# New rates and operand waits in the clock that paces a mixer's background work

## The chip, the cores and the metric

The kernel runs on one core of one Trainium2 chip. A core has a matrix engine (TensorE, PE in the rows), a vector engine (VectorE, DVE), a scalar engine (ScalarE, ACT), a general engine (GpSimd, POOL) and a queue that only issues transfers (SyncE, SP). Each engine works through its own instructions strictly in the order in which the program lists them, and waits on semaphores for the others. [...] The metric is the time of one execution in microseconds (us) on the device, the median of several runs.

## The reference, cut to what matters

One layer works on 256 frames of width 2048, in float32:

```
x = x + 1/2 * SwiGLU_1(RMSNorm(x))                  # D_FF = 5632
p = RMSNorm(x) @ W_in                               # one projection for both groups of heads
x = x + concat(rwkv7_mix(p), hgrn2_mix(p)) @ W_out
x = x + 1/2 * SwiGLU_2(RMSNorm(x))
out = RMSNorm(x)
```

`rwkv7_mix` (16 heads of 64) is a delta-rule recurrence over the frames, `S = S*w + sa (kk*a) + v k` with `sa = -S kk`, followed by a norm over each head, a bonus and a gate. `hgrn2_mix` (8 heads of 128) is a gated linear recurrence, followed by a norm over each head and a gate. Both run forward in time.

## The kernel before, in words

**Weights.** Every large product is float32 work made of float32r products. A weight tile of 128x1024 ("piece", 678 of them, 512 KB each) is loaded into `raw`, ScalarE casts it to `hi`, and `lo = raw - hi` is made by VectorE or by GpSimd. TensorE then runs 8 products of `hi` with 512 columns and 8 of `lo` with 256 columns into a tile `mm`. Four buffers each for `raw`, `hi` and `lo`; the split of a piece is listed five pieces ahead of its use. Pieces 0 to 263 are SwiGLU 1, 264 to 381 the projections of the mixer, 382 to 413 the output projection `W_out`, 414 to 677 SwiGLU 2.

**The mixer.** The recurrences don't wait for the whole projection. Four generators do them: `rwkv(hf)` for two halves of the RWKV heads (groups 0 and 1) and `hgrn(gi)` for two halves of the HGRN heads. A group of RWKV first makes its decays, keys and score tiles; then it solves a triangular system by 31 steps of two VectorE instructions each, the second of which needs the first (`state["chain"]`); then it passes four chunks of 64 frames, in which TensorE products and PSUM copies follow one another (product of the state and scores, copy by ScalarE, product with the inverse, copy by VectorE, update of the state, output); then come the norm over each head (two sums by TensorE, a square root, four reciprocals), the bonus (an addition by GpSimd), the gate and `put_y`, which leaves the operand of `W_out`. Their products go to tiles `ps` and stand on TensorE's queue between the large products.

**What sets the order.** The program is listed by a loop over units of one piece. After each unit, `poll` (line 311) lets the first two generators go on by one step, if their delay in ticks is over and if `max(V.until, S.until) <= model.now() + BEHIND` (line 313, BEHIND is 2500 ns). `V`, `S` and `G` wrap the engines: every call adds a cost to the engine's `until`, and notes when its output will be `ready`. `model.now()` is TensorE's own count of columns. `need` (line 186) holds a generator until the operands of its next products are ready by that count. `spare` (line 398) uses the two `until` values to give a `lo` to VectorE or to GpSimd. The pieces of `W_out` need the generators' results: `yop` (line 1000) and `add_acc` (line 1010) call `step_bg` over and over while a result isn't there, which makes every generator go on at once, without a large product between. Afterwards the framework's own scheduler may still move instructions past one another where data and buffers allow it.

Of the kernel before, what the change touches and what calls it, by code (L numbers as in the profile page):

```python
# [97 lines left out]
def names_of(xs):  # L98
    return [getattr(getattr(x, "tensor", x), "name", None) for x in xs if hasattr(x, "shape")]


class Model:

    RATE = {"vector": 1.04, "scalar": 0.83, "gpsimd": 2.6}
    FIXED = {"vector": 90, "scalar": 110, "gpsimd": 60, "tensor": 3}
    LATENCY = 200.0

    def __init__(self):  # L110
# [10 lines left out]
class Engine:  # L121
# [3 lines left out]
    def cost(self, op, n):  # L125
        rate = self.model.RATE[self.name]
        if op == "reciprocal":
            rate *= 6
        elif self.name == "vector" and op in ("tensor_copy", "tensor_scalar"):
            rate *= 0.6  # L130
        elif self.name == "gpsimd" and op == "memset":
            rate *= 0.2
        elif op == "dma_start":
            return 1000.0
        return self.model.FIXED[self.name] + rate * n

# [3 lines left out]
    def __getattr__(self, op):  # L140
        fn = getattr(self.engine, op)

        def call(*args, **kwargs):
            m = self.model
            cost = self.cost(op, math.prod(args[0].shape[1:]))
            begin = max(self.until, m.now())
            self.until = begin + cost
            done = max(begin, m.wait(*args)) + cost + m.LATENCY + (5000.0 if op == "dma_start" else 0.0)
            for n in names_of(args[:1]):
                m.ready[n] = done  # L150
            return fn(*args, **kwargs)  # L151

        return call
# [1202 lines left out]
```

## Time and profile before

| | |
|---|---|
| median of 3 runs | 2068.35 us (2067.53 to 2068.65) |
| the profiled execution | 2067.46 us, its span 2065.7 us |
| TensorE busy | 2023.5 us, 98% of the span |
| VectorE, ScalarE, GpSimd busy | 1375.6, 1010.6, 362.3 us |
| `lo` subtractions on VectorE and GpSimd | 615 and 70 in the trace |

The span is the time from the first to the last instruction. A busy time is the time in which an engine had an instruction in work. Where rows carry a bracket, it is the idle time ahead of them and what ended it. All helper calls share two lines, L151 (the wrapped engines) and L171 (the products), so rows are told apart by their tiles: `mm` are the large products, `ps` the generators' products, `t` most working tiles. A tile `t` or `b` in the rows stands for many buffers.

### The profile page before, as it was taken

How to read it: one execution, taken by the hardware profiler on the slowest of the kernel's cores; microseconds unless marked ns; L12 is line 12 of the kernel's file. 1: busy time of each engine (PE TensorE's matmuls, PEld its weight loads, DVE VectorE, ACT ScalarE, POOL GpSimd, SP SyncE). 2: the span in 40 equal slices, each digit the busy share in tenths (PEclk: the TensorE clock that was granted, in tenths of full speed). 3: DMA queues.
4: the chain of work that ended last, by engine and by line, in shares of the span. 5: the costliest groups of instructions: out<-in, count | busy, mean ns of one | idle time of the engine just before them, and what ended most of it. 6: DMA issues, size and time to landing. Idle time of an engine off the chain costs nothing.

```text
span 2065.7 us, 31617 instructions
## 1 busy us (share of the span) xinstructions
PE 2023.5 (98%) x12766; PEld 1764.1 (85%) x12766; DVE 1375.6 (67%) x1498; ACT 1010.6 (49%) x1199; POOL 362.3 (18%) x220
## 2 busy tenths in 40 slices
PE   9999999999999999999989899999999999999998
PEld 7888888888888888788868788888888888888887
DVE  7665565565556688986888668856555655555657
ACT  6444443444344466465556545544444344434434
POOL 1211110111011032322343104211111011101101
PEclk9999999999999999999999999999999999999999
DMA  7555555556555565443434435555555555555553
GB/s 260 194 187 191 187 186 191 190 188 190 187 188 189 186 229 177 153 135 126 131 117 150 148 111 177 192 189 188 184 193 188 189 188 190 188 190 187 190 187 120
DMA packets 106146, 368.33 MB, mean 178 GB/s; under 512 B 11632, under 2 KB 18032, under 8 KB 105744
## 3 DMA queue, kind: packets, MB, share of 16 engines
q1 hardware_dynamic: 104352, 359.97, 53.2%
q0 software_dynamic: 1104, 6.06, 0.8%
q8 instruction: 100, 1.64, 0.3%
q14 instruction: 46, 0.38, 0.1%
q10 hardware_dynamic: 544, 0.28, 0.0%
HBM read 362.08 MB, written 4.19 MB: 177 GB/s over the span
## 4 chain that ended last, share of the span: by engine, by line
PE 49%; DVE 3%; POOL 1%; issue 1%; ACT 0%; DVEq 0%; POOLq 0%; ACTq 0%
PE mm L171 45%; PE ps L171 4%; DVE t L151 2%; POOL t L151 1%; DVE lo L151 1%; ACT t L151 0%; DVE xts L151 0%; DVE b L151 0%; POOL lo L151 0%; PE ps L175 0%; POOL b L151 0%; ACT hi L151 0%; DVEq L1352 0%; ACT inv L151 0%; ACT itok L151 0%
## 5 line engine op out<-in xcount | busy, mean ns | idle before, releaser
L171 PE MATMUL mm<-t,hi 128*128 128x512 f32 x5264 | 1332.7, 394 | 3.7 <-DVE t L151 3.5
L151 ACT CAST hi<-raw 128x1024 fp32r<-128x1024 f32 (+1 forms) x685 | 711.1, 1040 | 882.6 <-PE mm L171 752.3
L171 PEld LDWEIGHTS mm<-t,hi 128*128 128x128 f32 x5264 | 948.5, 190 | 174.9 <-ACT hi L151 2.2
L151 DVE TENSOR_TENSOR lo<-raw,hi 128x1024 fp32r<-128x1024 f32 (+1 forms) x615 | 777.0, 1265 | 443.0 <-ACT hi L151 420.4
L171 PEld LDWEIGHTS mm<-t,lo 128*128 128x128 f32 x5296 | 727.7, 191 | 69.9 <-POOL lo L151 11.4
L171 PE MATMUL mm<-t,lo 128*128 128x256 f32 x5296 | 749.2, 284 | 13.0 <-POOL lo L151 10.5
L151 POOL TENSOR_TENSOR lo<-raw,hi 128x1024 fp32r<-128x1024 f32 x70 | 170.4, 2434 | 531.9 <-ACT hi L151 508.3
L151 POOL TENSOR_TENSOR t<-t,inv 128x1024 f32<-128x1024 f32 x22 | 53.0, 2407 | 777.8 <-ACT t L151 777.8
L151 DVE TENSOR_TENSOR t<-t,t 128x512 fp32r<-128x512 f32 (+25 forms) x243 | 171.6, 710 | 13.9 <-ACT t L151 7.6
L151 DVE TENSOR_TENSOR t<-mm,t 128x512 f32<-128x512 f32 x122 | 83.3, 683 | 88.9 <-ACT t L151 88.9
L151 DVE SCALAR_TENSOR_TENSOR xts<-mm,xts 128x512 f32<-128x512 f32 x126 | 86.6, 688 | 76.3 <-PE mm L171 75.9
L151 ACT COPY t<-mm 128x512 f32<-128x512 f32 x122 | 70.8, 580 | 16.2 <-DVE t L151 14.9
L151 ACT CAST t<-t 128x512 fp32r<-128x512 f32 x72 | 44.1, 622 | 27.2 <-DVE t L151 18.9
L151 DVE TENSOR_TENSOR t<-t,inv 128x1024 f32<-128x1024 f32 (+1 forms) x35 | 44.1, 1261 | 1.0
L151 DVE RECIPROCAL t<-t 128x256 f32<-128x256 f32 x24 | 41.4, 1737 | 2.4 <-ACT t L151 2.3
L151 ACT ACTIVATE t<-t 128x1024 f32<-128x1024 f32 (+2 forms) x32 | 32.9, 1028 | 12.8 <-DVE t L151 12.8
L151 POOL TENSOR_TENSOR t<-t,t 128x1024 f32<-128x1024 f32 (+1 forms) x9 | 25.4, 2820 | 73.2 <-ACT hi L151 45.0
L151 DVE SCALAR_TENSOR_TENSOR t<-xts,vec,t 128x256 fp32r<-128x256 f32 x48 | 25.9, 561 | 13.9 <-ACT t L151 13.9
L151 ACT ACTIVATE t<-xts,vec 128x256 fp32r<-128x256 f32 x48 | 23.0, 505 | 22.0 <-DVE xts L151 19.1
L151 ACT COPY t<-ps 32x512 f32<-32x512 f32 (+8 forms) x44 | 19.7, 447 | 27.4 <-PE ps L171 26.4
L171 PE MATMUL mm<-hi,t 128*128 128x512 f32 x128 | 32.4, 393 | 0.0
L151 ACT ACT_TABLE_LOAD x21 | 26.9, 1283 | 5.0 <-DMA xts<-in_xt_dram 3.4
(134 smaller groups left out, 713.6 us busy)
## 6 DMA issues: line engine op xcount, KB each, us to landing
raw<-in_ffn_w_up_dram SPq DMA_DIRECT2D x176, 512.0 KB, 3.4
raw<-in_ffn_w_down_dram SPq DMA_DIRECT2D x176, 512.0 KB, 3.3
raw<-in_ffn_w_gate_dram SPq DMA_DIRECT2D x173, 512.0 KB, 3.4
raw<-in_w_in_dram SPq DMA_DIRECT2D x96, 512.0 KB, 3.4
raw<-in_w_out_dram SPq DMA_DIRECT2D x32, 512.0 KB, 3.3
raw<-in_w_i_dram SPq DMA_DIRECT2D x16, 512.0 KB, 3.3
raw<-in_w_lora_dram SPq DMA_DIRECT2D x6, 512.0 KB, 3.4
spill<-xts POOLq DMA_DIRECT2D x1, 2048.0 KB, 10.1
```

Of the source, the lines that this page charges most:

```text
L151: return fn(*args, **kwargs)
L171: return self.engine.matmul(out, a, b, **kwargs)
```

## The change

The clock of VectorE, ScalarE and GpSimd is changed in three ways. The rates and fixed costs have other numbers; `tensor_reduce`, `tensor_tensor_scan` and `transpose` get their own factors, `tensor_copy` loses its discount, and a reduction is counted by its input. And a call (other than a transfer) now begins, in the clock, no sooner than its operands are ready, so that `until` takes in the wait; before, the wait only moved the output's `ready`. Nothing of the arithmetic is changed.

```diff
-    RATE = {"vector": 1.04, "scalar": 0.83, "gpsimd": 2.6}
-    FIXED = {"vector": 90, "scalar": 110, "gpsimd": 60, "tensor": 3}
+    RATE = {"vector": 1.1, "scalar": 0.87, "gpsimd": 2.4}
+    FIXED = {"vector": 130, "scalar": 160, "gpsimd": 100, "tensor": 3}
...
-            rate *= 6
-        elif self.name == "vector" and op in ("tensor_copy", "tensor_scalar"):
+            rate *= 5.7
+        elif op in ("tensor_reduce", "tensor_tensor_scan"):
+            rate *= 2
+        elif self.name == "vector" and op == "transpose":
+            rate *= 1.3
+        elif self.name == "vector" and op == "tensor_scalar":
             rate *= 0.6
...
-            cost = self.cost(op, math.prod(args[0].shape[1:]))
+            cost = self.cost(op, math.prod(args[op == "tensor_reduce"].shape[1:]))
+
             begin = max(self.until, m.now())
+            if op != "dma_start":
+                begin = max(begin, m.wait(*args[1:], *kwargs.values()))
             self.until = begin + cost
```

What the change moves is seen in the engines' own lists. The added lines shift the helper lines by seven (L151 is now L158, L171 is L178).

TensorE, group 1 of RWKV, where its triangular system is solved. `xts` holds the scores here, the first operand of the two 32x32 groups is the transposed result of the 31 steps, and each `mm` row is half of a piece's `hi` or `lo`. Before:

```order
L171 MATMUL ps<-t_10506,xts 32x32 x32
L171 MATMUL mm<-t_6148,lo 128x256 x2
L171 MATMUL mm<-t_6203,hi 128x512 x4
L171 MATMUL mm<-t_6255,hi 128x512 x4
L171 MATMUL mm<-t_6203,lo 128x256 x4
L171 MATMUL mm<-t_6255,lo 128x256 x4
L171 MATMUL mm<-t_6312,hi 128x512 x4
L171 MATMUL ps<-q_10446,t_10445 64x64 x4
L171 MATMUL ps<-q_10446,t_10445 64x65 x4
L171 MATMUL mm<-t_6364,hi 128x512 x4
L171 MATMUL mm<-t_6312,lo 128x256 x2
L171 MATMUL ps<-t_10507,t_10548 32x32 x32
```

And now:

```order
L178 MATMUL mm<-t_11103,lo 128x256 x4
L178 MATMUL mm<-t_11106,lo 128x256 x4
L178 MATMUL ps<-t_11171,xts 32x32 x32
L178 MATMUL ps<-t_11172,t_11175 32x32 x32
L178 MATMUL ps<-b_11077,xts 64x64 x8
L178 MATMUL ps<-t_11267,t_11100 64x64 x8
L178 MATMUL ps<-b_11077,b_10968 64x64 x8
L178 MATMUL ps<-xts,b_11077 64x64 x8
L178 MATMUL ps<-st_103,b_10763 64x128
```

Before, large products of the projection stand between these groups, at piece 374 and after it. Now they stand inside the output projection, behind pieces 398 and 399, and no large product follows until the gate of group 1 is through: 72 rows of `ps` with 224 products in a row. Before, the longest such run within the mixer has 37 products.

TensorE, group 0 of RWKV, at its gate (`t_6647` is the gate's activation). Before:

```order
L171 MATMUL mm<-t_6364,hi 128x512 x2
L171 MATMUL ps<-t_6647,t_6872 128x256 x4
L171 MATMUL ps<-t_6647,t_8377 128x256 x4
L171 MATMUL mm<-t_6364,hi 128x512 x2
```

And now, with the levels of group 1 of HGRN (`q`) ahead of the gate, and behind it the first large product that needs group 0's result (`t_10526`):

```order
L178 MATMUL ps<-t_6647,t_9939 128x256 x5
L178 MATMUL ps<-q_9281,t_10166 32x32 x32
L178 MATMUL ps<-q_10264,t_10263 32x32 x32
L178 MATMUL ps<-q_10311,t_10310 32x32 x32
L178 MATMUL ps<-q_10358,t_10357 32x32 x32
L178 MATMUL ps<-q_10405,t_10404 32x32 x32
L178 MATMUL ps<-q_10459,t_10458 32x32 x12
L178 MATMUL ps<-q_10459,t_10458 32x33 x4
L178 MATMUL ps<-t_6647,t_6908 128x256 x2
L178 MATMUL ps<-t_6647,t_9812 128x256 x2
L178 MATMUL mm<-t_10526,hi 128x512 x6
```

This is the end of a second such run, 60 rows with 284 products, at piece 383 (before, the gate of group 0 stood at piece 340, in the projections).

GpSimd, the end of the mixer. `xts` is now the residual, which comes back by a transfer from `spill` and takes four additions; the last row here is the bonus of RWKV group 1 (`t_10686` before, `t_11252` now). Before:

```order
L151 DMA xts<-spill 128x4096
L151 TENSOR_TENSOR xts<-t_11036,xts 128x1024
L151 TENSOR_TENSOR xts<-t_11205,xts 128x1024
L151 TENSOR_TENSOR lo<-raw,hi 128x1024
L151 TENSOR_TENSOR xts<-t_11326,xts 128x1024
L151 TENSOR_TENSOR t_10686<-t_10686,t_9702 128x1024
```

And now:

```order
L158 DMA xts<-spill 128x4096
L158 TENSOR_TENSOR t_11464<-t_11459,t_11464 128x2x256
L158 TENSOR_TENSOR xts<-t_10573,xts 128x1024
L158 TENSOR_TENSOR xts<-t_10683,xts 128x1024
L158 TENSOR_TENSOR xts<-t_10793,xts 128x1024
L158 TENSOR_TENSOR xts<-t_10927,xts 128x1024
L158 TENSOR_TENSOR t_11252<-t_11252,t_10894 128x1024
```

All four additions, where three stood before, are now ahead of the bonus. Over the whole program 110 `lo` subtractions move from VectorE to GpSimd (180 of them are listed there now, 70 before), most in the two SwiGLU stages, where GpSimd now makes four of every 16 pieces of gate and up (mostly two before) and one of every three of down (mostly one of 24 before).

## Rows read from the trace of the kernel before

**Rows 1.** Busy time by stage: stretch, length, then each engine, clock, DMA share, GB/s

```profile
800.00:1300.00 500.00, 472.12 (x3873) 398.86 (x3872) 406.43 (x540) 287.46 (x390) 152.87 (x114) 0.98 0.43 142
1300.00:2040.00 740.00, 740.00 (x4240) 651.22 (x4240) 450.15 (x427) 333.56 (x356) 92.31 (x39) 1.00 0.58 187
```

**Rows 2.** What TensorE waited for from 800 to 1300 us: total, times, longest

```profile
PE ps L171 <- DVE t L151: 11.0, 7, 6.8
PE mm L171 <- POOL lo L151: 10.5, 2, 6.9
```

**Rows 3.** Timeline of TensorE around its longest wait: start, length, instruction

```profile
1051.39 2.00 PE L171 MATMUL mm<-t,hi 128*128 128x512 f32 x8
1060.25 2.08 PE L171 MATMUL mm<-t,lo 128*128 128x256 f32 x8 [6.86 <-POOL lo L151]
1062.12 3.52 PE L171 MATMUL mm<-t,hi 128*128 128x512 f32 x8
1065.48 1.12 PE L171 MATMUL mm<-t,lo 128*128 128x256 f32 x8
```

**Rows 4.** Timeline of TensorE, products of one chunk of RWKV

```profile
1210.34 0.43 PE L171 MATMUL ps<-st,b 128*64 128x128 f32 x2
...
1211.97 0.40 PE L171 MATMUL ps<-b,xts 128*64 128x64 f32 x4
...
1213.20 1.14 PE L171 MATMUL ps<-t,t 64*64 64x64 f32 x16
...
1218.42 0.69 PE L171 MATMUL ps<-b,b 128*64 128x64 f32 x16
...
1221.29 0.34 PE L171 MATMUL ps<-xts,b 128*64 128x64 f32 x4
```

**Rows 5.** Groups of instructions by shape, 800 to 1300 us: count | busy, mean ns | idle

```profile
L151 DVE RECIPROCAL t<-t 128x256 f32<-128x256 f32 x24 | 41.4, 1737 | 2.4 <-ACT t L151 2.3
...
L151 POOL TENSOR_TENSOR t<-t,t 128x1024 f32<-128x1024 f32 x8 | 23.5, 2935 | 72.4 <-ACT hi L151 45.0 <-ACT t L151 14.2 <-DVE t L151 12.8
L151 DVE TENSOR_TENSOR t<-t,t 128x512 fp32r<-128x512 f32 x27 | 22.3, 851 | 7.8 <-ACT t L151 7.6
...
L151 ACT ACT_TABLE_LOAD x13 | 16.7, 1283 | 0.2
L151 ACT CAST t<-t 128x512 fp32r<-128x512 f32 x27 | 16.2, 623 | 11.7 <-POOL t L151 3.5 <-DVE b L151 3.5 <-DVE t L151 3.4
...
L151 POOL TENSOR_SCALAR t<-t,vec 128x256 f32<-128x256 f32 x16 | 13.9, 874 | 28.4 <-ACT t L151 20.2 <-DVE t L151 7.5 <-ACT hi L151 0.6
...
L151 ACT ACTIVATE t<-t 128x1024 f32<-128x1024 f32 x8 | 8.5, 1062 | 3.9 <-DVE t L151 3.8
...
L151 DVE COPY b<-ps 64x512 f32<-64x512 f32 x8 | 5.5, 689 | 4.3 <-PE ps L171 4.2
...
L151 ACT COPY t<-ps 64x512 f32<-64x512 f32 x8 | 4.6, 579 | 7.3 <-PE ps L171 7.3
```

**Rows 6.** Groups by shape, VectorE, 1128 to 1148 us: steps of the triangular solve

```profile
L151 DVE TENSOR_TENSOR t<-t,t 128x126 f32<-128x126 f32 x5 | 1.5, 291 | 0.1
...
L151 DVE TENSOR_TENSOR t<-t,t 128x16 f32<-128x16 f32 x2 | 0.3, 167 | 0.0
```

**Rows 7.** Timeline of GpSimd at the end of the mixer

```profile
1233.86 0.59 POOL L151 DMA_DIRECT2D xts<-spill  x1 [13.33 <-PE ps L171]
1242.40 5.97 POOL L151 TENSOR_TENSOR xts<-t,xts 128x1024 f32<-128x1024 f32 x2 [7.95 <-DMA xts<-spill]
...
1265.71 3.28 POOL L151 TENSOR_TENSOR t<-t,t 128x1024 f32<-128x1024 f32 x1 [5.45 <-DVE t L151]
```

**Rows 8.** Timeline of GpSimd and VectorE in SwiGLU 2

```profile
1431.51 2.41 POOL L151 TENSOR_TENSOR t<-t,inv 128x1024 f32<-128x1024 f32 x1 [24.12 <-ACT t L151]
...
1432.88 2.12 DVE L151 TENSOR_TENSOR lo<-raw,hi 128x1024 fp32r<-128x1024 f32 x1 [1.41 <-ACT hi L151]
...
1435.67 1.23 DVE L151 TENSOR_TENSOR lo<-raw,hi 128x1024 fp32r<-128x1024 f32 x1 [0.67 <-ACT hi L151]
```

## The prediction

> **What bounds the kernel now.** I first read busy time by stage. From 1300 to 2040 us TensorE is busy 740.00 of 740 us at full clock [rows 1]: the SwiGLU stages are TensorE and nothing else, and no reordering can make them shorter. From 800 to 1300 us, the mixer, it is busy 472.12 of 500 us, so 27.9 us are idle there. That is all an ordering clock can win back in the middle. The list of what TensorE waited for names the idle time: 11.0 us for a VectorE result of the generators (one wait of 6.8, the end of a triangular solve) and 10.5 us in two waits for a `lo` on GpSimd [rows 2]. The timeline shows that a long wait costs more than its length: after the 6.86 us gap eight `lo` products took 2.08 us instead of 1.12 and eight `hi` products 3.52 instead of 2.00, so TensorE ran at half clock and lost another 2.5 us [rows 3].
>
> **What the change moves.** The clock now holds VectorE's and ScalarE's `until` further ahead of TensorE's, since it takes in waits. `poll` lets a generator go on only while `until` is at most 2500 ns ahead, so the generators are let on less often, and everything of them comes later in the lists. The listing shows how late: the chunks of group 0 no longer stand in the projections but at piece 383, the solve and chunks of group 1 behind pieces 398 and 399. There the output projection needs the results, and the generators are driven to their end with no large product between: two runs, of 284 and 224 products of `ps`. A serial chain that lay beside large products now lies on TensorE's path. The question is what each costs.
>
> **A chunk.** State and score products run from 1210.34 to 1212.37, the inverse's take 1.14, the update's 0.69, the output's about 2.5, up to 1221.63 [rows 4]; between them stand a ScalarE copy of 0.58 and a VectorE copy of 0.69 [rows 5]. In series: 2.0 + 0.6 + 1.1 + 0.7 + 0.7 + 2.5 = 7.7 us, of which TensorE works 6.4; the last chunk, without the update, 7.0 and 5.7. So the chunks themselves idle TensorE by only 1.3 us each. The norms and the solve are dearer.
>
> **Run A, group 0 at piece 383.** Two chunks without large products: 14.7 us, TensorE 12.1. Then the norm, on one path: three table loads of ScalarE (3.9, one for group 1's square root that stands ahead), two wide passes (2.1), four casts (2.5), two splits (1.7) and six reciprocals (10.4, two of them group 1's) make 20.6 us [rows 5]. Behind them VectorE lists group 1's and HGRN's work, and GpSimd three 128x1024 products (8.8, the bonus last) and four of the scalings (3.5) [rows 5], with about eight level products of HGRN, 7 by an estimate at the 0.87 of a scaling: 19 us. Then a level, the gate's products, four VectorE products and the last split, all short: I take 8. Elapsed 14.7 + 20.6 + 19 + 8 = 62 us. TensorE has the two chunks and some 12 us of sums, levels and gate (an estimate: some ten groups of small products, each about the 1.1 us of the inverse's): 24. Idle: 38 us.
>
> **Run B, group 1 behind piece 399.** From the last scores: two reciprocals of HGRN (3.5 [rows 5]) and the copies and the transpose ahead of the solve (4, an estimate of six passes at the 0.6 to 0.7 of the copies in [rows 5]); 62 steps between 0.29 and 0.17 us [rows 6], 16 us by a mean of 0.26, with two splits (1.7) and one `lo` (1.2, [rows 8]) among them; transposes, two block products and copies, 8 by an estimate of a dozen such passes. That is 34 us. Four chunks: 4.7 for the first, which has no state, 7.7, 7.7 and 7.0, so 27. Then the norm: one wide pass, four casts, two splits, four reciprocals (1.1 + 2.5 + 1.7 + 7.0, [rows 5]) and 8 for sums, subtraction, root and scaling (again a dozen such passes): 20 us. Beside it GpSimd brings back the residual: the transfer can start when the last chunk has let go of the buffer, takes 8.5 us to its first use and then 3.0 us an addition [rows 7]. Four additions are now listed ahead of the bonus, so the bonus starts 0.6 + 8 + 12 = 20.6 us after the chunks, no later than the norm lets it; bonus 2.9, then gate and split 3. So 27 us. In all 34 + 27 + 27 = 88 us. TensorE has two pieces (16 products each at 740/4240 us, 5.6 us in all, [rows 1]), two block products (2.5), chunks (22) and sums with gate (5): 35. Idle: 53 us.
>
> **Clock.** Four gaps in these runs are longer than the 6.86 us after which half clock was seen: the norm of A, the start and the middle of the solve, the norm of B. At 2.5 us each, 10 us [rows 3].
>
> **What is won.** With steps held back longer, the projections run with fewer waits. Of the 27.9 us idle and of some 7 us of half clock after three large gaps I take 20 as gone: the 6.8 us wait for a solve has moved into the runs, one of two waits for a `lo` goes, and half of the small ones. The bounds are 35 (all gone) and 0, since GpSimd's list in the projections has the same pattern as where a `lo` came late (a `lo` behind eight scalings and two wide products) and twice as many `lo`.
>
> **The moved `lo`.** In a slice of SwiGLU, 16 pieces at 2.79 us or 44.6 us, GpSimd now has four `lo` and one product, five times 2.41 [rows 8]: 12 us. `hi` is cast four pieces ahead of use, so a `lo` that takes 1.2 us longer is early by several us still: 0. If the cover were gone, it would be 1.2 us for each of 110, 130 us; if VectorE's time were the bound, a gain. Neither is, with TensorE at 740 of 740. There is one price beside it: a `lo` on VectorE took 2.12 us instead of 1.23 while GpSimd ran a product [rows 8]. [...] In SwiGLU it changes nothing; in run B the additions may hold the norm's splits.
>
> The edits of the rates alone have no cost of their own: they act through the order only, as above.
>
> **Sum.** Profiled execution 2067.5 us + 38 + 53 + 10 - 20 = 2148.5 us. It lies 0.9 us below the median of the runs, within their spread; I say 2148 us.
>
> **Rivals.**
> 1. Only one run is exposed. The scheduler moved two pieces into run B; if VectorE and GpSimd run so far ahead of TensorE that A's norm is mostly done when TensorE comes to it, A's 38 us and two clock losses fall away: 2148 - 43 = 2105 us. For it: TensorE has 12 us of large products among A's first chunks. Against: TensorE's queue is in order, and the norm needs the last chunk's output. 12%.
> [...]
> 3. Not slower. The place is the middle: all of the 35 us are won, and each run idles TensorE by no more than the chunk copies and half of the solve, about 5 and 12 us, with one clock loss of 2.5: 2067 - 35 + 20 = 2052 us. It decides if the two runs together idle TensorE less than 35 us; my count is 91, and the norm's reciprocals alone are 7 us each in series. 4%.
> 4. It doesn't do what it says: the order hardly changes, 2068 us. The lists above exclude most of it. 1%.
>
> **How the numbers follow.** The forecast holds 65%, rival 1 12%, rival 2 18%, rivals 3 and 4 5%. The range of the likeliest comes from the won time (0 to 35, against 20), the estimates in the runs (27 us in all, by a third either way) and clock (5 to 15): 2125 to 2178. For 8 in 10 I reach to both neighbours: 2098 to 2188. A measurement of this kernel tells about 0.2%, 4 us, from no change. Faster by more: 0.03; within: 0.02; slower: 0.95.
>
> **What would show it.** In the profile after, TensorE should have two stretches after 1100 us with no large product, of about 62 and 88 us, busy for some 24 and 35 us of them, with half clock in parts; its waits should name VectorE's `t` and GpSimd's `t` or `xts`, and the critical chain should run through reciprocals and the solve's small products. The projections should have less idle time than 27.9 us. SwiGLU 2 should stay at 100% with GpSimd busier (some 190 to 215 us of 740, 47 more `lo` at 2.41 us on top of 92). I am wrong if TensorE is busy in both runs, or if a SwiGLU stage shows waits for a `lo` on GpSimd.

## The result, and the profile after

The kernel after takes 2155.61 us (median; 2153.70 to 2162.46), the one before 2068.19: a ratio of 1.0431, with a 95% interval of 1.0418 to 1.0444. 2148 us was forecast, with a range of 2098 to 2188. From the page before, and the head of the page after:

```profile
PE 2023.5 (98%) x12766; PEld 1764.1 (85%) x12766; DVE 1375.6 (67%) x1498; ACT 1010.6 (49%) x1199; POOL 362.3 (18%) x220
```

```profile
span 2152.8 us, 31657 instructions
PE 2052.7 (95%) x12766; PEld 1789.2 (83%) x12766; DVE 1274.2 (59%) x1383; ACT 1015.4 (47%) x1202; POOL 631.0 (29%) x335
PEclk9999999999999999999996875899999999999999
```

TensorE runs the same 12766 instructions, but is busy 2052.7 us where it was 2023.5. Nothing was added to it, so the 29.2 us more are the same products at a lower granted clock (0.965 of full speed on average, 0.993 before). Its idle time is 2152.8 - 2052.7 = 100.1 us; before it was 2065.7 - 2023.5 = 42.2. So the 87.1 us of span are 57.9 of idle time and 29.2 of clock. The stretches show where (columns as in [rows 1]):

```profile
800.00:1130.00 330.00, 321.18 (x2302) 276.10 (x2302) 250.70 (x294) 189.69 (x240) 105.46 (x73) 0.98 0.52 168
1130.00:1205.00 75.00, 46.99 (x632) 34.48 (x630) 52.04 (x66) 38.24 (x64) 34.40 (x34) 0.68 0.05 14
1205.00:1256.00 51.00, 49.71 (x321) 43.26 (x321) 31.86 (x38) 27.70 (x38) 7.57 (x4) 1.00 0.44 145
1256.00:1365.00 109.00, 62.07 (x502) 51.13 (x501) 55.79 (x112) 25.32 (x39) 23.87 (x15) 0.61 0.09 30
1365.00:2040.00 675.00, 675.00 (x3868) 594.02 (x3867) 369.81 (x346) 312.29 (x341) 192.42 (x80) 1.00 0.57 187
```

The second and the fourth row are the two runs: 28.0 and 46.9 us idle, at mean clocks of 0.68 and 0.61, with almost no transfers (5% and 9% of the DMA engines). The projections ahead of them have 8.8 us of idle time, against 27.9 in the mixer before [rows 1], and SwiGLU 2 is full. What TensorE waited for from 1130 to 1380 us names the engines:

```profile
PE mm L178 <- DVE t L158: 23.9, 4, 11.4
PE ps L178 <- ACT t L158: 21.6, 13, 6.3
PE ps L178 <- DVE t L158: 18.0, 4, 13.9
PE ps L178 <- POOL q L158: 7.5, 2, 4.4
```

The long waits are for results of the generators, two of them for the `t` that the output projection itself reads (`mm`). No wait for a `lo` is left among them. TensorE's timeline, first across run A, then across run B:

```profile
1135.10 0.74 PE L178 MATMUL mm<-t,lo 128*128 128x256 f32 x4
...
1178.51 1.08 PE L178 MATMUL ps<-q,t 128*32 128x32 f32 x64 [6.27 <-ACT t L158]
...
1189.42 1.08 PE L178 MATMUL ps<-q,t 128*32 128x32 f32 x64 [4.41 <-POOL q L158]
...
1202.30 2.56 PE L178 MATMUL mm<-t,hi 128*128 128x512 f32 x10 [0.75 <-DVE t L158]
...
1269.58 3.50 PE L178 MATMUL mm<-t,hi 128*128 128x512 f32 x8 [11.24 <-DVE t L158]
...
1290.72 1.92 PE L178 MATMUL ps<-t,xts 32*32 32x32 f32 x64 [13.89 <-DVE t L158]
...
1296.66 1.97 PE L178 MATMUL ps<-b,xts 128*64 128x64 f32 x16
...
1308.17 1.14 PE L178 MATMUL ps<-t,t 64*64 64x64 f32 x16 [0.72 <-ACT t L158]
1310.09 1.08 PE L178 MATMUL ps<-b,b 128*64 128x64 f32 x16 [0.78 <-DVE b L158]
...
1318.68 1.14 PE L178 MATMUL ps<-t,t 64*64 64x64 f32 x16 [0.71 <-ACT t L158]
...
1337.44 2.17 PE L178 MATMUL ps<-t,bones_r 128*128 128x512 f32 x4 [1.12 <-ACT t L158]
...
1360.71 3.78 PE L178 MATMUL mm<-t,hi 128*128 128x512 f32 x8 [11.44 <-DVE t L158]
```

From the last large product before run A (ending at 1135.8) to the next are 66.5 us; from the last scores (1258.3) to the large products behind run B 102.4 us. A chunk goes every 10.5 us (1308.17 to 1318.68), and its update took 1.08 us where [rows 4] have 0.69. The eight `hi` products behind the two long waits of `mm` take 3.50 and 3.78 us, at a granted clock of 0.57 (1269.58 to 1273.10) and 0.50 (1360.70 to 1364.50). Behind the gap of [rows 3] it was 0.50 (1060.25 to 1065.40).

The end of run B on VectorE, then on GpSimd, answers to [rows 5, 7]:

```profile
1344.80 6.59 DVE L158 RECIPROCAL t<-t 128x256 f32<-128x256 f32 x4 [1.83 <-ACT t L158]
...
1352.68 3.28 DVE L158 TENSOR_SCALAR t<-t,vec 128x256 f32<-128x256 f32 x4
```

```profile
1336.63 0.57 POOL L158 DMA_DIRECT2D xts<-spill  x1 [43.63 <-PE ps L178]
...
1344.62 10.23 POOL L158 TENSOR_TENSOR xts<-t,xts 128x1024 f32<-128x1024 f32 x4 [0.49 <-DMA xts<-spill]
1356.11 2.34 POOL L158 TENSOR_TENSOR t<-t,t 128x1024 f32<-128x1024 f32 x1 [1.26 <-DVE t L158]
```

The four additions are done at 1354.85, 1.3 us before the bonus can start: the bonus waits for VectorE, not for the residual itself. The last section shows what the additions did to VectorE.

### The profile page after: what moved, and what is told of

The parts are those of the page before. It is cut to its first block, busy times and chain, and to the rows that moved or that the text cites. A ratio compares the mean times of both kernels' runs of the same rounds, so it can differ in the third digit from the quotient of the medians.

```text
span 2152.8 us, 31657 instructions
## 1 busy us (share of the span) xinstructions
PE 2052.7 (95%) x12766; PEld 1789.2 (83%) x12766; DVE 1274.2 (59%) x1383; ACT 1015.4 (47%) x1202; POOL 631.0 (29%) x335
## 5 line engine op out<-in xcount | busy, mean ns | idle before, releaser
L178 PE MATMUL mm<-t,hi 128*128 128x512 f32 x5264 | 1330.9, 394 | 27.8 <-DVE t L158 27.3
L158 ACT CAST hi<-raw 128x1024 fp32r<-128x1024 f32 (+1 forms) x685 | 710.8, 1040 | 913.9 <-PE mm L178 865.2
L178 PEld LDWEIGHTS mm<-t,hi 128*128 128x128 f32 x5264 | 950.7, 190 | 200.0 <-DVE t L158 27.8
L158 DVE TENSOR_TENSOR lo<-raw,hi 128x1024 fp32r<-128x1024 f32 (+2 forms) x505 | 639.3, 1268 | 480.9 <-ACT hi L158 470.0
L178 PEld LDWEIGHTS mm<-t,lo 128*128 128x128 f32 x5296 | 725.2, 191 | 62.4 <-DVE lo L158 5.6
L178 PE MATMUL mm<-t,lo 128*128 128x256 f32 x5296 | 744.2, 283 | 7.5 <-DVE lo L158 3.9
L158 POOL TENSOR_TENSOR lo<-raw,hi 128x1024 fp32r<-128x1024 f32 x180 | 437.9, 2433 | 900.0 <-ACT hi L158 889.6
L158 DVE TENSOR_TENSOR t<-mm,t 128x512 f32<-128x512 f32 x122 | 83.5, 685 | 185.3 <-ACT t L158 185.2
L158 DVE TENSOR_TENSOR t<-t,t 128x512 f32<-128x512 f32 (+24 forms) x238 | 169.5, 715 | 17.7 <-ACT t L158 10.4
L158 DVE SCALAR_TENSOR_TENSOR xts<-mm,xts 128x512 f32<-128x512 f32 x126 | 86.9, 690 | 76.8 <-PE mm L178 74.8
L158 POOL TENSOR_TENSOR t<-t,inv 128x1024 f32<-128x1024 f32 x22 | 52.8, 2400 | 265.1 <-ACT t L158 265.1
L158 ACT COPY t<-mm 128x512 f32<-128x512 f32 x122 | 70.8, 581 | 11.6 <-DVE t L158 9.6
L158 ACT CAST t<-t 128x512 fp32r<-128x512 f32 x72 | 43.7, 621 | 31.3 <-DVE t L158 27.5
L178 PE MATMUL ps<-t,t 32*32 32x32 f32 (+5 forms) x352 | 39.9, 293 | 7.9 <-ACT t L158 5.6
L158 POOL TENSOR_TENSOR t<-t,t 128x1024 f32<-128x1024 f32 (+1 forms) x14 | 30.0, 2143 | 59.3 <-ACT t L158 52.2
L158 ACT COPY t<-ps 32x512 f32<-32x512 f32 (+8 forms) x44 | 19.3, 446 | 56.2 <-PE ps L178 55.6
L158 DVE RECIPROCAL t<-t 128x256 f32<-128x256 f32 x24 | 40.9, 1730 | 7.5 <-ACT t L158 7.5
L158 DVE TENSOR_TENSOR t<-t,inv 128x1024 f32<-128x1024 f32 (+1 forms) x35 | 44.6, 1275 | 1.1
L178 PEld LDWEIGHTS ps<-t,t 32*32 32x32 f32 (+4 forms) x352 | 29.4, 167 | 16.7 <-ACT t L158 6.8
L158 ACT ACTIVATE t<-t 128x1024 f32<-128x1024 f32 (+2 forms) x32 | 32.9, 1028 | 20.1 <-DVE t L158 20.0
L158 POOL TENSOR_TENSOR t<-t 128x1020 f32<-128x1020 f32 (+1 forms) x7 | 16.7, 2384 | 70.2 <-DVE t L158 66.8
L158 DVE SCALAR_TENSOR_TENSOR t<-xts,vec,t 128x256 fp32r<-128x256 f32 x48 | 26.9, 586 | 12.2 <-ACT t L158 12.2
```

What stands on the lines that cost most here:

```text
L178: return self.engine.matmul(out, a, b, **kwargs)
```

## The experiments

"Drawn" below are products that the program issues inside `step_bg`, when the output projection forces a generator on; the kernel after has 340 of them at piece 383 and 268 at 397. All but e5, e9 and e12 change only the order or the engine of a `lo`. A float32 product of the generators has two records in the trace, so that 32 listed ones stand there as x64, and four fillers as x8.

**e1: the rates alone.** The wait is taken out of after.

```
-            if op != "dma_start":
-                begin = max(begin, m.wait(*args[1:], *kwargs.values()))
```

> After with the operands' wait taken out again: the new rates and factors alone. In the order of its instructions the first run is gone (no ps product is drawn at piece 383) and the run behind piece 397 has 192 drawn products, against 340 and 268 with the waits; GpSimd takes 142 of the lo's, against 70 before and 180 after. My theory (the generators come late because the rough clock runs late; what is drawn without weight products beside it costs its chains' length): the run left is the chunks, the norm and the gate, some 70 us long with about 25 us of products at full clock, so +45, less some 15 won in the projections: 2100 us (2080 to 2120), and PE without a stretch of ps products alone at 1135-1202. Rival 'rates alone do it': 2150. [...] Rival 'only the waits matter': 2068.

2102.67 us, ratio 1.0166 (1.0150 to 1.0181). Run A is gone, and what is lost is in 1200:1400:

```profile
800.00:1200.00 400.00, 372.25 (x3027) 312.86 (x3027) 323.15 (x416) 233.44 (x318) 144.10 (x106) 0.97 0.41 138
1200.00:1400.00 200.00, 182.70 (x1242) 154.47 (x1241) 135.50 (x161) 90.96 (x118) 56.53 (x27) 0.91 0.42 143
```

The same stretches of before:

```profile
800.00:1200.00 400.00, 374.69 (x3245) 315.75 (x3243) 324.97 (x449) 236.98 (x325) 123.36 (x102) 0.97 0.42 136
1200.00:1400.00 200.00, 197.43 (x1205) 171.13 (x1204) 150.20 (x157) 102.70 (x125) 49.57 (x20) 1.00 0.53 175
```

In the second stretch e1 leaves TensorE idle for 17.3 us, before for 2.6, and the clock falls to 0.91; the first differs by 2.4. So taking out the operands' waits gives back some 53 of the 87 us, with run A gone; the rates alone cost some 35. Whether these 35 come by way of lateness too is what e3 asks.

**e2: only the places of the `lo`.** The clock of before, and for every piece the engine that after uses, from a written list.

```
+LO = ...               # one letter for each lo, V or G
...
-        eng = V if not 8 <= i < len(pieces) - 4 else spare(size)
+        eng = V if LO[state['nlo']] == 'V' else G
+        state['nlo'] += 1
```

> The kernel before, with its own rough clock for the generators, but every lo of a weight piece on the engine that the kernel after gives it (a written list; 180 on GpSimd instead of 70). In its order 8 ps products are drawn at piece 397, so the generators keep their pace. My theory: the places of the lo's did no harm and won the projections' idle time, so 2048 to 2062 us, with less than 12 us of PE idle at 800 to 1100 (27.9 in 800:1300 before). [...] Rival 'lo's change nothing either way': 2068.

2085.64 us, ratio 1.0087 (1.0072 to 1.0102). My expectation missed by some 30 us: the places did not win the idle time of the projections, they lost 18 us, with 8 products drawn. e7 and e8 ask where.

**e3: the rates, with the gate opened.** As e1, and `BEHIND = 12000.0`.

> The new rates and factors without the operands' wait, and BEHIND 12000 instead of 2500, so that the generators may be stepped while VectorE's and ScalarE's clocks stand up to 12 us ahead of TensorE's. No ps product is drawn in either run, and GpSimd takes 146 lo's. My theory: the time is that of before less what the lo's win in the projections: 2050 us (2040 to 2068), no stretch of ps products alone. Rival 'rates alone do it': 2150 still, since they are all there. [...]

2089.92 us, ratio 1.0108 (1.0091 to 1.0125), where I expected 2050. With nothing drawn the run is gone, but the time is not that of before:

```profile
800.00:1200.00 400.00, 360.72 (x3060) 303.36 (x3059) 322.42 (x422) 225.19 (x305) 150.02 (x113) 0.94 0.38 131
1200.00:1400.00 200.00, 197.76 (x1269) 171.37 (x1268) 151.95 (x153) 103.66 (x135) 61.66 (x25) 1.00 0.49 166
```

The idle time has moved from behind 1200 us (2.2 us are left) to ahead of it (39.3, against 27.8 in e1). From 780 to 1420 us TensorE waited 39.9 us, ahead of generators' and of large products alike, against 27.8 in before. Of the 35 us of e1 only 13 came back, so only these are shown to come from the run. The other 22 are close to the 18 that the places of the `lo` cost by themselves in e2, and e3 too has GpSimd make 146 of them; no run has the new rates with the places of before. Nor does any run open the gate with the waits kept: that the waits act through line 313 is argued from the listings.

**e4: the waits only behind SwiGLU 1.** The wait counts only once TensorE's rough clock is past 700 us.

```
+            if op != "dma_start" and m.pe > 700000:
```

> After, with the operands' wait counted only once TensorE's rough clock is past 700 us (the end of SwiGLU 1); up to there it is as in e1. The drawn products are 340 and 268 as in after. My theory: the waits that matter are those in the projections and the mixer; SwiGLU 1 has none of it: 2150 us (2140 to 2162), stretches of 66 and 102 us as after. Rival 'the waits of SwiGLU 1 and the places of its lo's carry part of the loss': 2100 to 2135.

2156.66 us, ratio 1.0430 (1.0410 to 1.0449): all of the loss. The waits that matter are those behind SwiGLU 1, so those of the projections and the mixer, as SwiGLU 2 leaves TensorE no idle time.

**e5: TensorE kept busy during the solve.** After, with 90 products of the identity with itself, whose result nothing reads, drawn in front of the solve's transposed products.

```
+    def fill(n):
+        w = ps1()
+        for _ in range(n):
+            nc.tensor.matmul(w[:, 0:P], ident, ident, start=True, stop=True)
...
+        if state.get("force"):
+            fill(90)
```

> After, with 90 products of the identity with itself (128x128, into a ps tile that nothing reads) put on TensorE where the drawn run of group 1 waits for its solve (1258 to 1290 us in after: waits of 11.2 and 13.9 us with 6.8 us of W_out products between). VectorE's solve doesn't depend on them. My theory: the half clock behind these waits is on the path, since the chunks are TensorE's own chain: they go every 10.5 us at half clock against 9.2 at full, the solve's products 5.4 us against about 3, the W_out and norm products lose some 4: 2141 us (2134 to 2150), granted clock near 1 from 1290 on. Rival 'the chain is set by VectorE and ScalarE whatever the clock': 2153 to 2158. Rival 'the fillers get in the way': over 2160.

2154.66 us, ratio 1.0421 (1.0406 to 1.0437): no difference from after. The stretches 1256:1290 and 1290:1340:

```profile
1256.00:1290.00 34.00, 30.18 (x245) 28.34 (x244) 30.30 (x79) 11.08 (x14) 5.05 (x3) 0.99 0.03 12
1290.00:1340.00 50.00, 40.88 (x423) 35.32 (x423) 11.34 (x22) 9.71 (x18) 4.89 (x6) 0.60 0.11 33
```

The clock was 0.99 during the solve and still 0.60 in the chunks behind it. So this run did not put the question that it was made for; e9 and e12 do.

**e6: lateness alone.** The kernel before, in which only the two generators of group 1 start later.

```
-        bg.append([g, clock[0] + 1, None, False])
+        bg.append([g, clock[0] + late, None, False])   # late: 60 for group 1, else 1
```

> The kernel before with its own rough clock; only the two generators of group 1 take their first step 60 ticks later than they are spawned. In its order 265 products are drawn behind piece 397 (268 in after) and none at 383, while GpSimd takes 69 lo's (70 before). My theory (lateness alone is what costs): after's second run cost 102 us less some 35 of products at full clock, 67; the projections win some 15 of their idle time, as no generator of group 1 is in them: 2068 + 67 - 15 = 2120 us (2100 to 2135), with a stretch of drawn products behind the scores of some 70 to 100 us. Rival 'the lo's or the rates cost it': 2068, neither is changed.

2113.22 us, ratio 1.0215 (1.0198 to 1.0232); expected 2120. The profiled execution is the longest of its four (2119.46):

```profile
800.00:1200.00 400.00, 376.38 (x2806) 320.41 (x2805) 317.12 (x398) 231.47 (x296) 111.84 (x84) 0.97 0.45 145
1200.00:1400.00 200.00, 167.97 (x1346) 141.47 (x1345) 131.84 (x181) 85.02 (x128) 48.50 (x33) 0.81 0.33 106
```

With the rates and the waits as in before, and 69 `lo` on GpSimd instead of 70, a run of 265 drawn products idles TensorE 32.0 us and takes the clock to 0.81. This is the mechanism of the forecast by itself.

**e7 and e8: e2 in two halves.** The list of e2 for the `lo` of both SwiGLUs only (e7), and for pieces 264 to 413 only (e8); the other half is before's.

> The kernel before with after's engine for the lo's of both SwiGLUs (150 of 528 on GpSimd, 54 before), and its own in pieces 264 to 413. Nothing is drawn. My theory: TensorE is busy for all of both SwiGLUs either way, so 2068 us (2064 to 2072). Rival 'the places in the SwiGLUs carry what e2 lost': 2086.

2070.02 us, ratio 1.0010 (1.0001 to 1.0020), as expected. The first row is SwiGLU 1, the second SwiGLU 2:

```profile
60.00:800.00 740.00, 740.00 (x4242) 651.32 (x4241) 406.97 (x395) 339.65 (x372) 207.03 (x91) 1.00 0.60 192
...
1300.00:2040.00 740.00, 740.00 (x4239) 651.14 (x4238) 398.47 (x375) 332.88 (x357) 211.72 (x88) 1.00 0.59 188
```

In SwiGLU 2 GpSimd works 211.72 us instead of 92.31 [rows 1], TensorE stays at 740.00.

> The kernel before with after's engine for the lo's of pieces 264 to 413 only (30 on GpSimd against 16, 30 of the 150 pieces differ), and its own in both SwiGLUs. 8 products are drawn at piece 397. My theory after e2: the 18 us that e2 lost are here, since GpSimd's lo's take 2.4 us instead of 1.2 and hold VectorE where products wait for either (lo waits of TensorE, VectorE's t): 2086 us (2080 to 2090). Rival 'SwiGLU lo's carry them': 2068.

2083.33 us, ratio 1.0074 (1.0059 to 1.0089): the loss of e2 is in the mixer. My reason for it, that GpSimd's `lo` are slow and hold VectorE, was not yet tested.

**e10: fewer `lo` on GpSimd in the mixer.** The kernel before, with VectorE for every `lo` while a generator lives.

```
-        return V if state["chain"] or late <= (1500.0 if bg else 0) else G
+        return V if state["chain"] or late <= (1000000.0 if bg else 0) else G
```

> The kernel before, with every lo split while a generator lives on VectorE (62 lo's on GpSimd instead of 70); 12 products are drawn at piece 397. My theory after e8 (14 more GpSimd lo's in pieces 264 to 413 cost 15 us): the reverse gives back TensorE's 10.5 us of waits for GpSimd's lo's less what VectorE is later by: 2061 us (2055 to 2067). Rival 'VectorE, busy 85 to 90% there, is then late with the generators': 2070 to 2080.

2085.45 us, ratio 1.0083 (1.0070 to 1.0097). TensorE's waits from 780 to 1420 us:

```profile
PE ps L171 <- DVE t L151: 15.8, 4, 10.8
PE mm L171 <- DVE t L151: 12.0, 3, 10.8
```

The waits for GpSimd's `lo` are gone, as wanted, and two waits of 10.8 us for VectorE stand in their place. With more `lo` on GpSimd in the mixer (e8) and with fewer the kernel loses the same 15 to 17 us. So it is not their number alone. Of my reason for e8, one half does not hold: there TensorE waited 7.4 us for a GpSimd `lo`, less than the 10.5 of before. The other half stays open: its waits for VectorE's results were 27.8 us in e8 (780 to 1420 us), against 16.6 in before.

**e11: the gate of before opened.** `BEHIND = 8000.0`, nothing else.

> The kernel before with BEHIND 8000 instead of 2500: the gate opens earlier, nothing is drawn in either, 75 lo's on GpSimd. My theory: before's generators keep their pace already, so that the gate is worth nothing more: 2068 us (2060 to 2074). Rival 'stepping earlier always helps': under 2060. Rival 'products stand in TensorE's queue ahead of their operands': over 2075.

2088.41 us, ratio 1.0094 (1.0079 to 1.0109), with nothing drawn. My theory (2068) missed by 20 us. TensorE's longest waits from 780 to 1420 us:

```profile
PE ps L171 <- DVE t L151: 14.2, 6, 5.4
PE ps L171 <- ACT t L151: 11.8, 5, 8.9
```

With the smaller ones it waited 33.1 us ahead of generators' products, against 13.8 in before, and 6.2 ahead of large ones, against 14.0. That is the rival of products that stand in the queue ahead of their operands.

**e9 and e12: fillers in the chunks.** As e5, and fillers where a chunk waits for a copy. e9 has four at three places of a chunk and 20 more at the solve, in both runs. e12 has the 90 of e5 and, in a chunk, two ahead of its second group and two ahead of the state's products, in run B alone (`hf` is 1 there); its expectation has these four at one place:

```
+            pr = ps1()
+            fill(pr, 2, hf)
...
+                pu = ps1()
+                fill(pu, 2, hf)
```

> After, with products of the identity with itself on TensorE wherever a drawn run waits in rwkv: 90 and 20 around the solve, and 4 (some 0.9 us) ahead of the second and third group of products of each chunk and of the last one, where it waits 0.7 to 0.8 us for a copy. e5 kept the clock at 0.99 up to 1290 us and it still stood at 0.60 in the chunks behind, so that it couldn't tell. My theory: if these fills bring the clock of the chunks back, run B's chunks go at 9.2 us instead of 10.5 and with the products of solve and norm some 10 to 13 us come back: 2143 us (2138 to 2150). Rival 'the chain is set by the copies whatever the clock': 2153 to 2160 with the clock near 1. If the clock stays near 0.6 again, the cost of the half clock stays open and the fills cost 0 to 10: 2155 to 2165.

2158.11 us, ratio 1.0435 (1.0419 to 1.0451). I expected 2143.

```profile
1300.00:1340.00 40.00, 40.00 (x440) 35.68 (x438) 7.44 (x15) 6.52 (x14) 0.57 (x1) 0.90 0.02 3
```

```profile
1295.00 1.99 PE L178 MATMUL ps<-t,xts 32*32 32x32 f32 x64 [4.71 <-DVE t L158]
```

The clock of the chunks came back to 0.90, a chunk went every 9.1 us, but with 3.5 us of fillers in it, and the solve's first products came at 1295.00 us, against 1290.72 in after. The fillers ahead of the solve did not hold it up, as TensorE still waited 4.71 us behind them. Run A had already ended late: the large products behind it came at 1208.73 instead of 1202.30, although its clock was 0.78 instead of 0.66 (1130 to 1200 us).

> As e9, with fewer fillers and only in group 1's drawn run: 90 in the waits around the solve, as in e5, and 4 in each chunk ahead of its second group of products. In e9 the clock of the chunks came back (0.90 at 1300 to 1340) and a chunk went every 9.1 us with 3.5 us of fillers in it, of which some 1.5 lay in waits, so that without the surplus it would take some 7.1 instead of 10.5 to 11.3. My theory (the half clock of run B is on the path): four chunks at about 8 us, so 10 to 12 us less: 2144 us (2139 to 2150). Rival 'what the chunks win is lost behind them, since the end waits for VectorE and GpSimd': 2153 to 2157. If the clock of 1300:1340 stays under 0.75, it tells nothing more than e5.

2149.84 us (2144.36 to 2153.70), ratio 1.0402 (1.0388 to 1.0416). The profiled execution, stretch 1290:1340 and two chunks:

```profile
1290.00:1340.00 50.00, 42.23 (x445) 34.64 (x439) 15.74 (x23) 13.07 (x23) 11.74 (x10) 0.76 0.16 57
```

```profile
1305.09 1.16 PE L232 MATMUL ps<-cst 128*128 128x128 f32 x8
1306.18 1.14 PE L178 MATMUL ps<-t,t 64*64 64x64 f32 x16
...
1308.10 0.69 PE L178 MATMUL ps<-b,b 128*64 128x64 f32 x16 [0.41 <-DVE b L158]
...
1312.67 1.16 PE L232 MATMUL ps<-cst 128*128 128x128 f32 x8
1313.76 1.14 PE L178 MATMUL ps<-t,t 64*64 64x64 f32 x16
...
1350.52 3.78 PE L178 MATMUL mm<-t,hi 128*128 128x512 f32 x8 [11.49 <-DVE t L158]
```

A chunk goes every 7.58 us instead of 10.5, although 1.16 us of useless products are in it, its update takes 0.69 us again, and the large products behind run B start at 1350.52 instead of 1360.71. In the profiles 10.2 us come back, in the medians 5.8; the profiled execution is the shortest of five, and the longest equals the shortest of after. So the low clock of run B's chunks (0.57 from 1290 to 1340 us in after, 0.76 here) was on the path, for 6 to 10 us. What the lost clock of run A and of the solve's and norm's products costs stays open: e9 raised run A's clock, but the run got longer with it.

## Why the prediction was right

**The mechanism was right.** Products of the generators that stood beside large products now stand alone, in the two runs at the places named. e6 makes such a run by lateness alone, e1 takes run A away with the waits, e3 takes the rest of run B away with the gate, and e4 shows in which stages the waits matter. Rival 1 (one run) fell with the rows 1130:1205 and 1256:1365, rivals 3 and 4 with the time, and rival 2 (longer runs, 2175 us) lay 19 us too high: the runs are 4.5 and 14 us longer than forecast, but in run B not by the norm: the norm with all behind it took 24.4 us (1336.3 to 1360.71), under the 27 forecast, and the residual's additions took 2.56 each, under the 3.0 of [rows 7]. It is the chunks that grew, 39.7 us (1296.66 to 1336.3) instead of 27, at a mean clock of 0.59, and largely by it, as e12 shows, with 4.3 more for what stands ahead of them. For run A no run shows what its 4.5 us are.

**The terms of the sum.** Run A: 62 us elapsed were forecast, 66.5 measured, but 28.0 idle instead of 38. Run B: 88 against 102.4 elapsed, 46.9 idle instead of 53. So TensorE was busy for 94 us in the two, where 59 were forecast. Won idle time ahead: 20 forecast with its clock, 27.9 - 8.8 = 19.1 measured.

**The step that was mis-sized is the clock.** I counted four long gaps at 2.5 us each, 10 us, as if the clock came back soon after each gap. It came back soon behind the gap of [rows 3], where large products follow (1.12 us for eight `lo` at 1065.48, and a clock of 1.00 from 1067 to 1075 us); in the runs small products of the generators follow, and the clock stayed at 0.68 and 0.61 on average. TensorE was busy 29.2 us more, not 10. Small products at these clocks fill time that I had counted as idle. The runs' idle time is 16 us under the forecast (74.9 against 91) and the clock's cost 19 us over it, which nearly cancel: 28.0 + 46.9 + 1.3 (between the runs) - 19.1 + 29.2 = 86.3 of the 87.1 us. That the sum was closer than its terms is luck.

Fillers raised the clock of run B's chunks: 0.57 at 1290 to 1340 us in after, 0.76 in e12, and 0.90 at 1300 to 1340 in e9. TensorE counted as busy for 41 of those 50 us in after and for 42 in e12, so busy time in the profile does not by itself tell the clock. What sets it is not shown here.

**The moved `lo` in SwiGLU cost next to nothing,** where the forecast had nothing: e7 shows 740.00 of 740 us in both and 2070.02 us, 2 us more than before by the medians.

**What I did not see.** The idle time of the projections is not there for the taking. e2, e3, e8, e10 and e11 change the mixer's order in five ways, with 0 to 12 products drawn, and lose 15 to 22 us each; the rows of e10 show one wait put in the place of another. The 19 us that after won ahead of its runs came only together with the runs. Before's order is the best of all that ran; which of its details does it is open. No version here beats before.

## What to carry to other kernels

A planner's clock that is made more truthful about one thing changes every decision that was tuned with the old one: count what it will hold back, and for a serial chain ask what stands beside it once it is late. The chains that had no large product beside them cost here their length, their waits and the clock of their own small products: 0.68 and 0.61 in the two runs, 1.00 behind each, from 1205 to 1256 and from 1365 us on. A remaining bit of idle time in a tuned order is not a reserve: five other orders all had more.

## What was not expected of the hardware

TensorE's granted clock stayed low with TensorE in use: at a mean of 0.57 from 1290 to 1340 us while it counted as busy for 41.46 of 50 us with the small products of the chunks:

```profile
1290.00:1340.00 50.00, 41.46 (x420) 35.86 (x420) 10.42 (x20) 9.71 (x18) 2.61 (x5) 0.57 0.06 15
```

A clock of 0.99 from 1256 to 1290 us (e5) left it at 0.60 behind, and products that compute nothing, put into the chunks, shortened them from 10.5 to 7.58 us (e12).

VectorE's four scalings at 1352.68 took 3.28 us, most of it while GpSimd still added the residual. In the mixer of before eight of them took 405 ns each on average. In e10, which has three of the additions ahead of the bonus, GpSimd was through with them and with a `lo` at 1283.40, and the same four took 1.38 us:

```profile
L151 DVE TENSOR_SCALAR t<-t,vec 128x256 f32<-128x256 f32 x8 | 2.8, 405 | 0.0
```

```profile
1280.07 3.33 POOL L151 TENSOR_TENSOR lo<-raw,hi 128x1024 fp32r<-128x1024 f32 x1
...
1284.52 1.38 DVE L151 TENSOR_SCALAR t<-t,vec 128x256 f32<-128x256 f32 x4
```

In before four took 1.46 us (0.74 for two at 1262.52 and 0.72 for two at 1264.91) while GpSimd was idle, and in e12 the four took 3.28 us again (at 1342.49), with GpSimd at the additions until 1344.65. So these scalings took longer beside the additions, as the `lo` of [rows 8] took 2.12 us instead of 1.23 beside a product. VectorE's product just ahead of them, at 1351.42, did not: 1.23 us beside the same additions, 1.21 in before (at 1261.27) with GpSimd idle. By an estimate from these rows (3.28 - 1.38) the additions held up the bonus of run B by some 1.9 us, through VectorE's scalings. The forecast had looked for this in the norm's splits, but those ran ahead of the additions. What in the chip does it is not shown.
